# Add-residual RMSNorm on one core: three fixed 64 KiB slots per partition, 8 rows per tile, and every transfer in one queue in a fixed order

## The chip, the cores and the metric

The kernel runs on one core of one Trainium2 chip. The time is that of the device in microseconds (us). The profile shows one execution; its span is about 2 us shorter than the measured time (3762.5 against 3764.65 us before, 3732.7 against 3734.45 us after). Lower is better. A core has a VectorE (DVE in the profile), a ScalarE (ACT), a GpSimd (POOL), a SyncE (SP, which only issues transfers here) and 16 DMA engines by the profile's page, whose queue table has all 1612 MB that the kernel before moves.

## The reference

```python
x        : (32, 2048, 2048) float32        # 65536 rows of 2048
residual : (32, 2048, 2048) float32
gamma    : (2048,) float32, all ones;  eps = 1e-6

z   = x + residual
rms = sqrt(mean(z ** 2, axis=-1, keepdims=True) + eps)
out = z / rms * gamma
```

Each of the three large tensors has 536.87 MB. Each is moved once, so any kernel moves 1610.6 MB.

## The kernel before

A tile is 128 partitions of 2 consecutive rows: 16 KB per partition, 2 MB in all, 256 tiles. Loads are issued by SP, stores by ScalarE; pools of 6 and 4 buffers decide when a load may start.

```python
R = 2
x_t = x_f.rearrange("(n p r) m -> n p r m", p=P, r=R)        # r_t and o_t alike
...
nc.sync.dma_start(out=gamma_tile, in_=gamma.partition_broadcast(P))      # 1 MB
...
xio = ctx.enter_context(tc.tile_pool(name="xio", bufs=6))
rio = ctx.enter_context(tc.tile_pool(name="rio", bufs=4))
...
for i in range(n_tiles):
    x_tile = xio.tile([P, R, D], fp32)
    r_tile = rio.tile([P, R, D], fp32)
    nc.sync.dma_start(out=x_tile, in_=x_t[i])
    nc.sync.dma_start(out=r_tile, in_=r_t[i])
    nc.vector.tensor_add(out=x_tile, in0=x_tile, in1=r_tile)
    for g in range(R):
        nc.scalar.activation(out=sq_junk, in_=x_tile[:, g, :], func=Square,
                             accum_out=ssq[:, g : g + 1])
    ...  # rms = Sqrt(ssq / D + eps) on ScalarE, rstd = 1 / rms on VectorE
    for g in range(R):
        nc.vector.scalar_tensor_tensor(   # row * rstd * gamma, in place
            ...)
    nc.scalar.dma_start(out=o_t[i], in_=x_tile)
```

## Time and profile before

| | before |
|---|---|
| time, median of 4 runs | 3764.65 us (3764.07 to 3765.12) |
| bytes moved, by the queue table | 1611.96 MB |
| VectorE busy, ScalarE busy | 62%, 29% |
| DMA engines | at 9 tenths or more in 39 of 40 slices |

From the profile's page of the kernel before: the span, VectorE's and ScalarE's busy time, the DMA share and the rate in 40 equal slices, the DMA queues (packets, MB, share of the 16 engines), and the chain of waits by engine.

```profile
span 3762.5 us, 4011 instructions
DVE 2322.1 (62%) x1025; ACT 1103.6 (29%) x1282; POOL 0.2 (0%) x4
...
DMA  9999999999999999999999999999999999999998
GB/s 416 431 430 431 431 430 431 430 431 430 430 431 431 430 431 431 431 431 430 431 431 430 431 431 431 430 431 431 430 431 430 431 431 430 431 430 431 430 431 356
DMA packets 110767, 1611.96 MB, mean 428 GB/s; under 512 B 12304, under 2 KB 12304, under 8 KB 12304
...
q1 hardware_dynamic: 73872, 1074.82, 66.9%
q10 hardware_dynamic: 36864, 536.89, 33.3%
q14 instruction: 31, 0.25, 0.0%
...
DMA 91%; DVE 8%; issue 1%; SPq 0%; ACT 0%; DVEq 0%
```

The kernel is bound by its transfers from the second slice to the last but one, at a flat 430 to 431 GB/s. Only the first and the last slice are below that. q1 is the queue of the loads, q10 that of the stores, and q14 brings the engines' instructions, a quarter of a megabyte in 31 packets of 8 KB.

The end, in the table by stretches: from and to in us, length, busy us of each engine, clock, DMA share, GB/s.

```profile
60.00:200.00 140.00, 85.18 (x39) 38.79 (x46) 0.00 (x0) 1.00 1.01 431
...
3725.00:3730.00 5.00, 2.15 (x1) 0.00 (x0) 0.00 (x0) 1.00 0.96 413
3730.00:3735.00 5.00, 4.96 (x4) 2.66 (x3) 0.00 (x0) 1.00 0.19 82
3735.00:3740.00 5.00, 4.96 (x4) 1.64 (x3) 0.00 (x0) 1.00 0.59 249
3740.00:3745.00 5.00, 5.00 (x2) 0.00 (x0) 0.00 (x0) 1.00 1.01 429
3745.00:3750.00 5.00, 1.05 (x1) 3.88 (x4) 0.00 (x0) 1.00 0.55 236
3750.00:3755.00 5.00, 4.48 (x3) 0.42 (x3) 0.00 (x0) 1.00 0.00 0
3755.00:3762.50 7.50, 0.30 (x1) 0.00 (x0) 0.00 (x0) 1.00 0.66 280
```

The last 35 us hold about 16 us of missing transfer: 5 x (1 - 82/431) is 4 us in the stretch from 3730, and so on down the list. The timeline of the same end shows the adds of the last two tiles and the last store being issued (start, duration, what, and in brackets the idle time before it and what ended it):

```profile
3727.84 4.42 DVE L56 TENSOR_TENSOR x_tile<-x_tile,r_tile 128x4096 f32<-128x4096 f32 x1 [8.00 <-DMA r_tile<-in_residual_dram]
...
3741.64 4.42 DVE L56 TENSOR_TENSOR x_tile<-x_tile,r_tile 128x4096 f32<-128x4096 f32 x1
...
3755.33 0.34 ACTq L89 DMA_DIRECT2D out_dram<-x_tile  x1
```

From the last add to the last store there are 13.7 us of compute.

### The profile page before, as it was taken

What the parts mean: (1) busy time and instruction counts of PE and PEld (TensorE: products, weight loads), DVE (VectorE), ACT (ScalarE), POOL (GpSimd) and SP (SyncE); (2) the same over time, 40 slices, a digit from 0 to 9 for tenths busy, and PEclk for the clock granted to TensorE, in tenths of its full rate; (3) what the DMA queues carried; (4) which work ended last, traced back from release to release, by engine and by line L of the source; (5) the groups of instructions that cost most, each with busy time, mean ns of one, the idle gap of its engine ahead of it and who ended that gap; (6) DMA issues with size and microseconds to landing.
All of it is one profiled execution on the core that took longest, in us unless ns stands there. A gap on an engine that the chain in (4) does not pass through costs nothing.

```text
span 3762.5 us, 4011 instructions
## 1 busy us (share of the span) xinstructions
DVE 2322.1 (62%) x1025; ACT 1103.6 (29%) x1282; POOL 0.2 (0%) x4
## 2 busy tenths in 40 slices
DVE  5566656666566655666566655666556665566656
ACT  3232322323223232322323232232323222232322
POOL 0000000000000000000000000000000000000000
DMA  9999999999999999999999999999999999999998
GB/s 416 431 430 431 431 430 431 430 431 430 430 431 431 430 431 431 431 431 430 431 431 430 431 431 431 430 431 431 430 431 430 431 431 430 431 430 431 430 431 356
DMA packets 110767, 1611.96 MB, mean 428 GB/s; under 512 B 12304, under 2 KB 12304, under 8 KB 12304
## 3 DMA queue, kind: packets, MB, share of 16 engines
q1 hardware_dynamic: 73872, 1074.82, 66.9%
q10 hardware_dynamic: 36864, 536.89, 33.3%
q14 instruction: 31, 0.25, 0.0%
HBM read 1074.79 MB, written 536.87 MB: 428 GB/s over the span
## 4 chain that ended last, share of the span: by engine, by line
DMA 91%; DVE 8%; issue 1%; SPq 0%; ACT 0%; DVEq 0%
DMA r_tile<-in_residual_dram 53%; DMA x_tile<-in_x_dram 22%; DMA out_dram<-x_tile 15%; DVE x_tile L80 5%; DVE x_tile L56 3%; SPq L53 0%; ACT sq_junk L61 0%; DVE rstd L77 0%; DVEq L120 0%; SPq L54 0%; DVEq L56 0%; SPq L41 0%; ACT rms L69 0%
## 5 line engine op out<-in xcount | busy, mean ns | idle before, releaser
L56 DVE TENSOR_TENSOR x_tile<-x_tile,r_tile 128x4096 f32<-128x4096 f32 x256 | 1132.0, 4422 | 1413.1 <-DMA r_tile<-in_residual_dram 1413.0
L61 ACT ACTIVATE sq_junk<-x_tile 128x2048 f32<-128x2048 f32 x512 | 963.3, 1881 | 2637.9 <-DVE x_tile L56 2629.9
L80 DVE SCALAR_TENSOR_TENSOR x_tile<-x_tile,rstd,gamma_tile 128x2048 f32<-128x2048 f32 x512 | 1181.4, 2349 | 9.1
L61 ACT ACTIVATION_READ_ACCUMULATOR sq_junk<-x_tile 128x1 f32 x512 | 95.4, 186 | 0.0
L69 ACT ACTIVATE rms<-ssq,eps_tile 128x2 f32<-128x2 f32 x256 | 75.7, 296 | 8.2
L77 DVE RECIPROCAL rstd<-rms 128x2 f32<-128x2 f32 x256 | 40.3, 158 | 10.1 <-ACT rms L69 10.1
L61 ACT ACT_TABLE_LOAD x1 | 1.3, 1283 | 0.7 <-PEq L106 0.7
L69 ACT ACT_TABLE_LOAD x1 | 1.3, 1283 | 0.0
L43 DVE MEMSET eps_tile<- 128x1 f32 x1 | 0.1, 59 | 0.8 <-PEq L106 0.8
L106 POOL MEMSET const-uint8-127<- 128x1 uint8 x1 | 0.1, 102 | 0.0
L106 POOL MEMSET const-bfloat16-1.0<- 128x1 bf16 x1 | 0.1, 101 | 0.0
L106 POOL MEMSET const-float32-0.0<- 128x1 f32 x1 | 0.1, 98 | 0.2 <-issue 0.2
L106 POOL MEMSET const-float32-1.0<- 128x1 f32 x1 | 0.1, 98 | 0.0
## 6 DMA issues: line engine op xcount, KB each, us to landing
x_tile<-in_x_dram SPq DMA_DIRECT2D x256, 2048.0 KB, 34.3
r_tile<-in_residual_dram SPq DMA_DIRECT2D x256, 2048.0 KB, 37.3
out_dram<-x_tile ACTq DMA_DIRECT2D x256, 2048.0 KB, 14.4
gamma_tile<-in_gamma_dram SPq DMA_DIRECT2D x1, 1024.0 KB, 4.3
```

The source lines that it names most:

```text
L43: nc.vector.memset(eps_tile, float(eps))
L56: nc.vector.tensor_add(out=x_tile, in0=x_tile, in1=r_tile)
L61: nc.scalar.activation(out=sq_junk, in_=x_tile[:, g, :], func=mybir.ActivationFunctionType.Square, accum_out=ssq[:, g : g + 1],)
L69: nc.scalar.activation(out=rms, in_=ssq, func=mybir.ActivationFunctionType.Sqrt, bias=eps_tile, scale=inv_d,)
L77: nc.vector.reciprocal(out=rstd, in_=rms)
L80: nc.vector.scalar_tensor_tensor(out=x_tile[:, g, :], in0=x_tile[:, g, :], scalar=rstd[:, g : g + 1], in1=gamma_tile, op0=mybir.AluOpType. ...
L106: nc = _bacc.Bacc("TRN2", target_bir_lowering=False, num_devices=1)
```

## The change: its intent and the diff

The intent is to keep the 16 DMA engines busy with fewer and longer transfers, and to shorten the end. A tile becomes 8 rows, 64 KB per partition and 8 MB. There are two slots for z (x is loaded there, and the result is computed in place) and one for the residual. All large transfers go through SP's queue in the order store(i-1), residual(i+1), x(i+1): while one transfer runs, the wait that the next one needs has time to end. gamma is loaded into four partitions and spread over the others by VectorE.

```diff
-    R = 2
+    R = 8
+    H = R // 2
...
+    z_slots = [slots.tile([P, R, D], fp32, name=f"z{k}") for k in range(2)]
+    r_slot = slots.tile([P, R, D], fp32, name="r_slot")
...
-    xio = ctx.enter_context(tc.tile_pool(name="xio", bufs=6))
-    rio = ctx.enter_context(tc.tile_pool(name="rio", bufs=4))
+    def load_r(i):
+        nc.sync.dma_start(out=r_slot, in_=r_t[i])
+    def load_x(i):
+        z = z_slots[i % 2]
+        for h in range(2):
+            s = slice(h * H, (h + 1) * H)
+            nc.sync.dma_start(out=z[:, s, :], in_=x_t[i][:, s, :])
+    def store(i):               # whole tile; the last tile in two halves
+        ...
+    def compute(i):             # add, square, rms by halves; then scale by halves
+        ...
+    def load_gamma():
+        nc.vector.memset(gamma_tile, 0.0)
+        for q in range(4):
+            nc.scalar.dma_start(out=gamma_tile[32 * q : 32 * q + 1, :],
+                                in_=gamma.partition_broadcast(1))
+        nc.vector.stream_shuffle(gamma_tile, gamma_tile, [0] * 32)
...
+    load_r(0)
+    load_x(0)
+    load_gamma()
+    load_x(1)
+    compute(0)
+    load_r(1)
+    for i in range(1, n_tiles):
+        store(i - 1)
+        compute(i)
+        if i + 1 < n_tiles:
+            load_r(i + 1)
+            load_x(i + 1)
+    store(n_tiles - 1)
```

More of the change, by code (lines that the diff above doesn't have):

```diff
@@ L22 @@
     fp32 = mybir.dt.float32
+    Act = mybir.ActivationFunctionType
+    mult = mybir.AluOpType.mult
     x_f = x.flatten_outer_dims()
@@ L28 @@
     n_rows, D = x_f.shape
-    R = 2
+    R = 8
+    H = R // 2
     assert n_rows % (P * R) == 0
     n_tiles = n_rows // (P * R)
+    assert n_tiles >= 3
     x_t = x_f.rearrange("(n p r) m -> n p r m", p=P, r=R)
@@ L37 @@
     inv_d = 1.0 / float(D)
-    singles = ctx.enter_context(tc.tile_pool(name="singles", bufs=1))
-    gamma_tile = singles.tile([P, D], fp32)
-    nc.sync.dma_start(out=gamma_tile, in_=gamma.partition_broadcast(P))
-    eps_tile = singles.tile([P, 1], fp32)
-    nc.vector.memset(eps_tile, float(eps))
-    xio = ctx.enter_context(tc.tile_pool(name="xio", bufs=6))
-    rio = ctx.enter_context(tc.tile_pool(name="rio", bufs=4))
-    stats = ctx.enter_context(tc.tile_pool(name="stats", bufs=8))
-    psum = ctx.enter_context(tc.tile_pool(name="psum", bufs=1, space=bass.MemoryType.PSUM))
@@ L50 @@
-    for i in range(n_tiles):
-        x_tile = xio.tile([P, R, D], fp32)
-        r_tile = rio.tile([P, R, D], fp32)
-        nc.sync.dma_start(out=x_tile, in_=x_t[i])
-        nc.sync.dma_start(out=r_tile, in_=r_t[i])
-        nc.vector.tensor_add(out=x_tile, in0=x_tile, in1=r_tile)
-        sq_junk = psum.tile([P, D], fp32)
-        ssq = stats.tile([P, R], fp32)
-        for g in range(R):
-            nc.scalar.activation(
-                out=sq_junk,
-                in_=x_tile[:, g, :],
-                func=mybir.ActivationFunctionType.Square,
-                accum_out=ssq[:, g : g + 1],
-            )
-        rms = stats.tile([P, R], fp32)
-        nc.scalar.activation(
-            out=rms,
-            in_=ssq,
-            func=mybir.ActivationFunctionType.Sqrt,
-            bias=eps_tile,
-            scale=inv_d,
-        )
-        rstd = stats.tile([P, R], fp32)
-        nc.vector.reciprocal(out=rstd, in_=rms)
-        for g in range(R):
-            nc.vector.scalar_tensor_tensor(
-                out=x_tile[:, g, :],
-                in0=x_tile[:, g, :],
-                scalar=rstd[:, g : g + 1],
-                in1=gamma_tile,
-                op0=mybir.AluOpType.mult,
-                op1=mybir.AluOpType.mult,
-            )
-        nc.scalar.dma_start(out=o_t[i], in_=x_tile)
@@ new lines @@
+    slots = ctx.enter_context(tc.tile_pool(name="slots", bufs=1))
+    stats = ctx.enter_context(tc.tile_pool(name="stats", bufs=3))
+    psum = ctx.enter_context(tc.tile_pool(name="psum", bufs=1, space=bass.MemoryType.PSUM))
+    z_slots = [slots.tile([P, R, D], fp32, name=f"z{k}") for k in range(2)]
+    r_slot = slots.tile([P, R, D], fp32, name="r_slot")
+    gamma_tile = slots.tile([P, D], fp32, name="gamma_tile")
+    eps_tile = slots.tile([P, 1], fp32, name="eps_tile")
+    sq_junk = psum.tile([P, D], fp32, name="sq_junk")
@@ new lines @@
+    nc.vector.memset(eps_tile, float(eps))
+    def load_r(i):
[6 more added lines that the diff above has]
+    def store(i):
+        z = z_slots[i % 2]
+        if i < n_tiles - 1:
+            nc.sync.dma_start(out=o_t[i], in_=z)
+            return
+        for h in range(2):
+            s = slice(h * H, (h + 1) * H)
+            nc.sync.dma_start(out=o_t[i][:, s, :], in_=z[:, s, :])
@@ new lines, in compute @@
+    def compute(i):
+        z = z_slots[i % 2]
+        rstds = []
+        for h in range(2):
+            s = slice(h * H, (h + 1) * H)
+            nc.vector.tensor_add(out=z[:, s, :], in0=z[:, s, :], in1=r_slot[:, s, :])
+            ssq = stats.tile([P, H], fp32, name=f"ssq{h}")
+            for g in range(H):
+                nc.scalar.activation(
+                    out=sq_junk,
+                    in_=z[:, h * H + g, :],
+                    func=Act.Square,
+                    accum_out=ssq[:, g : g + 1],
+                )
+            rms = stats.tile([P, H], fp32, name=f"rms{h}")
+            nc.scalar.activation(out=rms, in_=ssq, func=Act.Sqrt, bias=eps_tile, scale=inv_d)
+            rstds.append((rms, stats.tile([P, H], fp32, name=f"rstd{h}")))
+        for h in range(2):
+            rms, rstd = rstds[h]
+            nc.vector.reciprocal(out=rstd, in_=rms)
+            for g in range(H):
+                row = z[:, h * H + g, :]
+                nc.vector.scalar_tensor_tensor(
+                    out=row,
+                    in0=row,
+                    scalar=rstd[:, g : g + 1],
+                    in1=gamma_tile,
+                    op0=mult,
+                    op1=mult,
+                )
@@ new lines, in load_gamma @@
+    def load_gamma():
+        nc.vector.memset(gamma_tile, 0.0)
+        for q in range(4):
+            nc.scalar.dma_start(
+                out=gamma_tile[32 * q : 32 * q + 1, :], in_=gamma.partition_broadcast(1)
+            )
+        nc.vector.stream_shuffle(gamma_tile, gamma_tile, [0] * 32)
[11 more added lines that the diff above has]
+            load_x(i + 1)
```

## The prediction

> **What bounds it now.** The transfers. The page's slices show the 16 DMA engines at 9 tenths or more in 39 of 40 slices, moving 430 to 431 GB/s from the second slice to the last but one; VectorE is busy 62%, ScalarE 29%. VectorE's idle time (1413 us) waits for the residual load. The chain of waits is 91% DMA. [...]
>
> **What isn't at full rate.** (a) Start: the stretches show the first bytes at about 1.8 us. (b) End: the last slice has 356 GB/s, a loss of about 16 us against 431. The timeline shows why: the last 2 MB tiles are added, squared and scaled after all loads are done, with gaps between stores (82 GB/s at 3730 to 3735 us, none at 3750 to 3755). (c) gamma costs 1 MB, 2.4 us. [...]
>
> **What the change does.**
> - gamma: four 8 KB loads instead of 1 MB: about -2.4 us. Memset and shuffle run while the first 16 MB load; free.
> - Transfers of 8 MB (residual, output) and 4 MB (x halves): 256 instead of 769. [...] steady rate 431 -> 433 to 434 GB/s; -20 to -25 us. My least certain gain.
> - End: the last loads are followed in the queue by the store of tile 62 (19.4 us), under which the last tile is added and half scaled. Estimate from durations: second add ends about 11 us after the last load ([...]add 2 x 4.42), four scalings (4 x 2.32) end at about 20 us, so the first half store starts 2 to 3 us late, the second nearly without gap[...]. Tail loss about 4 instead of 16 us.
> - Compute per tile: VectorE 17.7 + 18.8 = 36.5 us, ScalarE about 17 us, under 58.1 us of transfers.
> - Fixed order with three slots: the next residual needs both adds, ready about 11 us after x lands, while the store in front takes 19.4 us. x's slot needs the store landed, while the residual load takes 19.4 us. The queue should never run dry.
>
> Sum: transfers 3714 to 3721, start 2, end 4, and 2.2 us between span and time: about 3726 us (-1.0%).
>
> **Chances.** Range 3706 to 3765. Faster by over 2%: 0.01; within 2%: 0.93; slower: 0.06.
>
> **What would show it.** Last slice near 430 GB/s; steady slices 433 to 434; packets down to a third or fewer; ScalarE's queue nearly empty; VectorE still 62%, its idle time in few, long waits for x.
>
> **What would make it wrong.** [...] If the steady 431 GB/s doesn't depend on transfer size, the gain shrinks to 15 us. If pieces of 64 KB spaced over 8 MB suit the HBM worse, or the engines drift apart by over 8 us, the residual load comes late and the rate falls below 431.

## The result, and the profile after

| | before | after |
|---|---|---|
| time, median of 4 runs | 3764.65 us | 3734.47 us (3733.57 to 3734.64) |
| ratio to before, 95% interval | | 0.992 (0.9906 to 0.9934) |
| span of the profile | 3762.5 us | 3732.7 us |

The change saves 30 us, 0.8%: within 2%, as predicted; the predicted time was 3726 us, 8.5 us too low and inside its range. A ratio here is the mean time of one kernel's fast runs over that of the other's of the same rounds, so not quite the ratio of the medians that are quoted.

The same lines of the page after (page, kernel after):

```profile
span 3732.7 us, 2427 instructions
DVE 2298.0 (62%) x772; ACT 1066.4 (29%) x1154; POOL 0.2 (0%) x4
...
GB/s 425 414 437 430 435 433 431 435 435 432 433 431 435 436 430 437 429 436 433 431 436 430 437 432 431 437 430 439 430 432 434 432 437 431 430 435 436 431 435 389
DMA packets 37035, 1610.82 MB, mean 432 GB/s; under 512 B 4116, under 2 KB 4116, under 8 KB 4116
...
q1 hardware_dynamic: 37008, 1610.63, 99.9%
q14 instruction: 19, 0.16, 0.0%
```

The slices now move about 433 GB/s, with a third of the packets. Two slices stand out, the second (414) and the last (389). The table by stretches, kernel after:

```profile
60.00:200.00 140.00, 90.81 (x31) 33.53 (x37) 0.00 (x0) 1.00 1.00 423
...
150.00:3650.00 3500.00, 2159.32 (x726) 1004.82 (x1087) 0.00 (x0) 1.00 1.00 433
...
3700.00:3705.00 5.00, 4.96 (x4) 3.71 (x4) 0.00 (x0) 1.00 0.61 262
3705.00:3710.00 5.00, 5.00 (x3) 4.90 (x7) 0.00 (x0) 1.00 0.15 66
3710.00:3715.00 5.00, 4.96 (x4) 0.00 (x0) 0.00 (x0) 1.00 0.74 315
3715.00:3720.00 5.00, 5.00 (x3) 0.00 (x0) 0.00 (x0) 1.00 0.97 419
3720.00:3725.00 5.00, 0.04 (x1) 0.00 (x0) 0.00 (x0) 1.00 0.98 419
3725.00:3732.70 7.70, 0.00 (x0) 0.00 (x0) 0.00 (x0) 1.00 0.79 340
```

Between 60 and 200 us the rate is 423 and not 433, a loss of about 3 us that the kernel before does not have there. And the end has a hole of some 8 us from 3702 to 3712.

A sum for both kernels makes the shares visible. The steady rate is worked out from the trace's packets that end between 200 and 3600 us (their bytes over 3400 us); bytes over that rate is the time that the transfers need; the rest of the span is start and end. A packet of the kernel after carries up to 64 KB, so its rate is good to about 0.1 GB/s and its sums to about 1 us.

| | bytes | steady rate | transfers | rest of the span |
|---|---|---|---|---|
| before | 1611.96 MB | 430.6 GB/s | 3743.2 us | 19.3 us |
| after | 1610.82 MB | 433.1 GB/s | 3719.0 us | 13.7 us |
| difference | | | -24.2 us | -5.6 us |
| predicted for after | | 433 to 434 | 3714 to 3721 us | 6 us |

So the rate came as predicted, and nearly all that was missed is in start and end.

**What the landings say.** Each large transfer leaves 16 semaphore records in the trace, and the queue table has 16 packets under 512 B for each (12304 for 769 transfers before). They are read here as one record of each DMA engine, at the time when its share has landed. So read, they show something that no view of the page shows: how far the engines stand apart. These are the largest lags behind the median engine in a stretch of the trace (from and to in us, about), for the slowest four engines, in us (worked out from those records):

```
                   slowest   2nd   3rd   4th
before  1000-1500      8.0   7.4   7.2   0.9
before  3500-3720     19.7  19.6  18.5   1.8
after   1000-1500      4.5   2.7   2.3   1.7
after   3500-3720      7.7   6.7   5.3   1.4
```

Three of the 16 engines fall behind steadily, in both kernels. In the kernel before they are up to 19.7 us late in the last stretch, and 13.6 us for the very last load. That is the 82 GB/s: 13 engines had finished their loads by 3729 us, and three still loaded until 3740.5. In the kernel after, the three are 5 to 8 us late, and they are what fills the stretch at 66 GB/s.

From about 830 us on, the lag of the slowest engine of the kernel after doesn't grow evenly. It steps by nearly 1 us, each time within a few us of a packet of the instruction queue. The first four of six such steps:

```
instruction packet at   slowest engine's lag, transfer before -> after it
 837 us                 2.6 -> 3.5
1351 us                 3.6 -> 4.5
1932 us                 4.6 -> 5.5
2514 us                 5.5 -> 6.4
```

The last three are 581 us apart, ten tiles of 58.1 us, in which VectorE is given about 120 instructions. Before 837 us the lag had grown to 2.6 us without a step of that size, so these packets go with most of the 7.7 us, not with all of it. Another engine steps by about 0.6 us at ScalarE's rhythm; a third drifts by about 0.1 us per tile with no steps.

From here there were these theories:

- *Pieces*: the steady rate rose because an engine's share is cut into fewer contiguous pieces. Rivals: fewer transfers; or the single queue.
- *Slowest engine*: the end is set by the DMA engine that is furthest behind, and the lag comes from instruction fetches. Rivals: the end is set by the compute of the last tile (the reading of the prediction); or fetches cost nothing.
- *Start*: the missing 3 to 4 us near 100 us come from the order of the first loads. Rival: a gap at the start is hidden by the lag at the end.

### The profile page after: what moved, and what is told of

It reads as the page before. It is cut to its first block, busy times and chain, and to the rows that moved or that the text cites. A ratio compares the mean times of both kernels' runs of the same rounds, so it can differ in the third digit from the quotient of the medians.

```text
span 3732.7 us, 2427 instructions
## 1 busy us (share of the span) xinstructions
DVE 2298.0 (62%) x772; ACT 1066.4 (29%) x1154; POOL 0.2 (0%) x4
## 2 busy tenths in 40 slices
DMA packets 37035, 1610.82 MB, mean 432 GB/s; under 512 B 4116, under 2 KB 4116, under 8 KB 4116
## 4 chain that ended last, share of the span: by engine, by line
DMA 66%; another core or an unknown queue 16%; DVE 16%; SPq 1%; ACT 0%; issue 0%; DVEq 0%
DMA z<-in_x_dram 64%; DVE z L80 15%; DMA out_dram<-z 1%; DVE z L97 1%; DMA r_slot<-in_residual_dram 1%; SPq L64 1%; SPq L58 0%; ACT sq_junk L83 0%; DVE rstd L94 0%; DVEq L158 0%; ACT L90 0%; ACT rms L90 0%; DVEq L80 0%
## 5 line engine op out<-in xcount | busy, mean ns | idle before, releaser
L80 DVE TENSOR_TENSOR z<-z,r_slot 128x8192 f32<-128x8192 f32 x128 | 1112.5, 8692 | 1395.0 <-DMA z<-in_x_dram 1382.5
L83 ACT ACTIVATE sq_junk<-z 128x2048 f32<-128x2048 f32 x512 | 963.5, 1882 | 2635.0 <-DVE z L80 2622.9
L97 DVE SCALAR_TENSOR_TENSOR z<-z,rstd,gamma_tile 128x2048 f32<-128x2048 f32 x512 | 1169.9, 2348 | 4.5
L83 ACT ACTIVATION_READ_ACCUMULATOR sq_junk<-z 128x1 f32 x512 | 95.8, 187 | 0.0
L90 ACT ACTIVATE rms<-ssq,eps_tile 128x4 f32<-128x4 f32 x128 | 38.1, 298 | 4.1
L94 DVE RECIPROCAL rstd<-rms 128x4 f32<-128x4 f32 x128 | 21.9, 171 | 0.1
```

The costliest lines, as they stand in the source:

```text
L80: nc.vector.tensor_add(out=z[:, s, :], in0=z[:, s, :], in1=r_slot[:, s, :])
L83: nc.scalar.activation(out=sq_junk, in_=z[:, h * H + g, :], func=Act.Square, accum_out=ssq[:, g : g + 1],)
L90: nc.scalar.activation(out=rms, in_=ssq, func=Act.Sqrt, bias=eps_tile, scale=inv_d)
L94: nc.vector.reciprocal(out=rstd, in_=rms)
L97: nc.vector.scalar_tensor_tensor(out=row, in0=row, scalar=rstd[:, g : g + 1], in1=gamma_tile, op0=mult, op1=mult,)
```

## The experiments

All of them gave correct results.

### e1_gamma: the gamma part alone, on the kernel before

```diff
-    nc.sync.dma_start(out=gamma_tile, in_=gamma.partition_broadcast(P))
+    nc.vector.memset(gamma_tile, 0.0)
+    for q in range(4):
+        nc.scalar.dma_start(out=gamma_tile[32 * q : 32 * q + 1, :],
+                            in_=gamma.partition_broadcast(1))
+    nc.vector.stream_shuffle(gamma_tile, gamma_tile, [0] * 32)
```

> The kernel before with the stream shuffle for gamma alone. Theory: it saves the 1 MB broadcast, 2.4 us at 431 GB/s, and nothing else: about 3762.3 us. Rival: the shuffle part is worth more because the first tile starts late behind it: 5 us or more.

Measured: 3763.44 us against 3764.53 us before in the same rounds, 1.1 us less (ratio 0.9997, interval 0.9982 to 1.0012). The gamma part is worth about one microsecond of the thirty. Less than the 2.4 us came through, and 1.1 us is no more than the spread of e1's own runs (1.7 us).

### e2_pieces16 and e3_transfers2m: pieces or transfers

e2 keeps the changed kernel's transfers and their order, but gives a partition four pairs of rows that lie apart in memory, so that each 8 MB transfer has pieces of 16 KB. e3 keeps the layout, and cuts each transfer into ones of 2 MB, which have pieces of 16 KB too.

```diff
# e2_pieces16 (x_t, r_t and o_t; the SBUF side is viewed alike)
-    x_t = x_f.rearrange("(n p r) m -> n p r m", p=P, r=R)
+    x_t = x_f.rearrange("(n a p b) m -> n p a (b m)", a=R // 2, p=P, b=2)
# e3_transfers2m (load_r; load_x and store alike)
-        nc.sync.dma_start(out=r_slot, in_=r_t[i])
+        for j in range(0, R, 2):
+            nc.sync.dma_start(out=r_slot[:, j : j + 2, :], in_=r_t[i][:, j : j + 2, :])
```

> The changed kernel with the same transfers (8 and 4 MB, same order, same queue), but each cut into contiguous pieces of 16 KB in memory instead of 64 and 32 KB. Theory (cost per piece): the steady rate falls from 433 to about 431 GB/s, as before; time 3744 to 3751 us. Rival (cost per transfer, or the order of the queue): steady rate stays 433, time 3734 +- 2 us.

> The changed kernel with each transfer cut into 2 MB transfers of 16 KB pieces, same order in the same queue. If the cost is per piece: as the run with 16 KB pieces in large transfers, at most 5 us slower[...]. If the cost is per transfer: this one alone is slow (3745 us or more), the other not.

Measured: e2 3759.38 us (ratio 0.9987), e3 3764.91 us (ratio 1.0001). One stretch of each, in the table by stretches; first e2, then e3:

```profile
150.00:3650.00 3500.00, 2135.14 (x720) 988.77 (x1071) 0.00 (x0) 1.00 1.01 430
```

```profile
150.00:3650.00 3500.00, 2133.41 (x719) 988.76 (x1071) 0.00 (x0) 1.00 1.01 430
...
3725.00:3730.00 5.00, 5.00 (x1) 4.94 (x5) 0.00 (x0) 1.00 0.26 111
3730.00:3735.00 5.00, 4.96 (x4) 3.62 (x6) 0.00 (x0) 1.00 0.11 46
```

With 16 KB pieces the rate is 430 again, though the transfers are as long and as few as in the changed kernel. So the rate belongs to the pieces, not to the number of transfers or to the single queue. How the pieces lie in HBM seems to matter little: in e2 and in the kernel before, the pieces of neighbouring partitions follow one another, in e3 they lie 64 KB apart, and the rates are 430.2, 430.7 and 430.2 GB/s. What an engine does between two pieces, these runs don't show. The change itself couldn't tell pieces from transfers, as it makes both fewer by a factor of three.

The effect was larger than expected: 24.9 us instead of 10 to 17 (runs of different rounds; the kernel before took 3764.19 to 3764.65 us in all of them). An engine moves 32 pieces per tile in the changed kernel (8 of the residual, 16 of x, 8 of the result) and 96 in e2. Over 64 tiles that is 4096 more, so each costs 6.1 ns by this estimate. That is a hundredth of the 0.61 us that 16 KB take an engine at 1/16 of 430 GB/s.

e3 is 5.5 us slower still, a little over the author's estimate of 5 us at most, at the same steady rate. Its trace shows the slowest engine 16.6 us behind at the end, and e2's 7.3 us; e3 has 28 packets of instructions, e2 has 20. Its end has the long hole at 111 and 46 GB/s.

### e4_two_queues: the stores from ScalarE's queue

```diff
-            nc.sync.dma_start(out=o_t[i], in_=z)
+            nc.scalar.dma_start(out=o_t[i], in_=z)
```

> The changed kernel with the stores issued from ScalarE's queue instead of the one fixed queue. Theory (the store's place in the queue fills the time in which the next residual load waits for the adds): without it the DMA engines have nothing queued for about 12 us of each tile, the tile takes about 70 us instead of 58, time 4300 to 4600 us, with gaps in GB/s. Rival (which queue issues a transfer doesn't matter): 3734 +- 10 us.

Measured, one look: 4211.8 us, 477 us (13%) slower than the changed kernel, somewhat less than the 4300 to 4600 us expected. SP's own waits in e4 (who waited for whom, us in total, times, longest):

```profile
SPq L64 <- DMA out_dram<-z: 3469.2, 62, 57.8
SPq L58 <- DVE rstd L94: 546.6, 63, 27.8
```

My expectation named the wrong wait. The residual load's wait for the adds is short. The long one is that of the x load (L64) for the store out of its slot: 3469 us, where the kernel after has this:

```profile
SPq L58 <- DVE rstd L94: 1772.3, 63, 29.3
...
SPq L64 <- DMA out_dram<-z: 625.9, 62, 10.5
```

From its own queue, a store of e4 shares the engines with the loads. The one issued at 2035.4 us shared them with the end of a residual load (landed at 2043.6) and then with half of an x load; it landed at 2069.7 and that half at 2070.1. The next half of x was issued at 2069.7, with nothing left in front of it. The stretches of e4 show such a hole one tile earlier:

```profile
2005.00:2010.00 5.00, 1.81 (x1) 0.00 (x0) 0.00 (x0) 1.00 0.43 131
2010.00:2015.00 5.00, 5.00 (x1) 0.00 (x0) 0.00 (x0) 1.00 0.87 374
```

In the one queue the store comes first and lands while the residual load still runs (kernel after: the store by 2025.8 us on the last engine, the residual load by 2045.2). The edit did one thing more than its line says: the scheduler now puts half of the next x load before the residual load in SP's queue (the add at 2043.6 us follows a residual load issued at 2016.9, and the half of x that it adds to was issued before that, at 2008.4). So e4 shows that with three slots the order of service matters; it doesn't show what the store's queue alone is worth. The rate gained nothing from the second queue: e4 moved 383 GB/s from 100 to 3650 us. But the choice also changed the order of service, and here the two together cost 477 us.

### e5_tail_quarters: the last tile in quarters

```diff
+    def compute_last(i):        # add, square, rms, reciprocal, scale for rows 0-1, then 2-3, ...
+        ...
-        for h in range(2):
-            s = slice(h * H, (h + 1) * H)
+        for h in range(4):
+            s = slice(h * 2, (h + 1) * 2)
             nc.sync.dma_start(out=o_t[i][:, s, :], in_=z[:, s, :])
```

> The changed kernel, but the last tile is added, squared, scaled and stored in quarters, so that its first store can start about 8 us earlier. Theory (the run ends when the slowest DMA engine has done its share; that engine has no gap at the end, only the fast ones have): time falls by at most 2 us. Rival (the chain of the last tile's compute delays the end, as predicted): time falls by 5 to 8 us.

Measured: 3734.74 us (ratio 0.9921), the same as the changed kernel. The stretches at its end:

```profile
3700.00:3705.00 5.00, 5.00 (x3) 3.37 (x3) 0.00 (x0) 1.00 0.81 351
3705.00:3710.00 5.00, 5.00 (x3) 0.93 (x3) 0.00 (x0) 1.00 0.95 406
...
3725.00:3730.00 5.00, 0.00 (x0) 0.00 (x0) 0.00 (x0) 1.00 0.27 115
3730.00:3735.00 5.00, 0.00 (x0) 0.00 (x0) 0.00 (x0) 1.00 0.02 7
```

The hole at 66 GB/s is filled: 406. And not a microsecond is won. The missing rate turns up at the very end, 115 and then 7 GB/s, when most engines are done and the late ones still store: by the landings, 12 engines are done at 3726.2 us and the slowest at 3731.8, where the changed kernel ends as well (3731.7). So a shorter compute of the last tile wins nothing; the slowest DMA engine holds the end where it is.

In the changed kernel that engine works on both sides of the compute. The last add waits for its landing (timeline, kernel after):

```profile
3692.83 8.69 DVE L80 TENSOR_TENSOR z<-z,r_slot 128x8192 f32<-128x8192 f32 x1 [0.99 <-DMA z<-in_x_dram]
```

The median engine's share of that load had landed at 3685.0 us, the slowest's at 3692.8. From there the compute took 18.0 us to the first half store (issued at 3710.8), while the slowest engine was still at the store in front of it (landed at 3712.1). Its share of the half store landed 9.8 us later, hardly more than the 9.7 us that 4 MB take at 433 GB/s: it had no gap. The compute and the slowest engine were ready for the half store at nearly the same time, so shortening the compute alone can't help.

### e6_pool4096, e7_dve32 and e7b_dve16: more instructions that nothing waits for

```diff
# e6_pool4096
+    for _ in range(4096):
+        nc.gpsimd.memset(idle_tile, 0.0)
# e7_dve32, at the head of compute(i)
+        for _ in range(32):
+            nc.vector.memset(idle_tile, 0.0)
# e7b_dve16, behind each of a tile's two reciprocals
+            for _ in range(8):
+                nc.vector.tensor_copy(out=idle_tile, in_=rstd[:, 0:1])
```

> The changed kernel with 4096 one-element memsets on GpSimd, which does nothing else and which nothing waits for. Theory (instructions are fetched in pieces of 8 KB through the same DMA engines, and each fetch holds up one engine by 0.5 to 1 us): 32 more packets in the instruction queue, one DMA engine lags by 16 to 32 us, time +8 to +25 us. Rival (fetches cost nothing; the lag belongs to certain DMA engines): time within 2 us of 3734.5, spread of landings still about 8 us.

> The changed kernel with 32 one-element memsets per tile on VectorE, at a place where it is idle (2048 in all, about 2 us of VectorE per tile). Theory (fetches): 16 more packets in the instruction queue, the lag of VectorE's DMA engine grows from 8 to about 24 us, time +10 to +17 us. Rival: VectorE has 21 us of slack per tile, so time stays within 2 us of 3734.5.

> Mend of the run with 32 memsets, which the scheduler had moved in bunches ahead of the adds: here 16 one-element copies per tile stand behind the reciprocals by their data, 1024 in all, about 1.5 us of VectorE per tile, which has 21 us of slack. Theory (fetches): 8 more packets in the instruction queue, VectorE's DMA engine lags by about 8 us more (15 at the end instead of 7 to 8), time +6 to +9 us. Rival: time within 2 us of 3734.5 and the same lag.

Measured: e6 3753.12 us, e7b 3742.07 us; the changed kernel has 3734.47. The instruction queue of e6 and of e7b, against 19 packets in the changed kernel:

```profile
q14 instruction: 51, 0.42, 0.0%
```

```profile
q14 instruction: 27, 0.22, 0.0%
```

In e6, 32 more packets cost 18.6 us, 0.58 us each, though GpSimd does nothing for the result and VectorE's busy time stayed at 2298.0 us. The time came as expected, the lag didn't: instead of one engine 16 to 32 us late, the slowest was 11.5 us late at most, and 6.2 us at the end. The trace shows why. GpSimd ran all its memsets at once, from 0.7 to 642.5 us, with a packet about every 20 us. Between 144 and 318 us nine of them passed, and the slowest engine's lag rose from 3.0 to 8.1 us, 0.6 us for each, while all others stayed within 1.6 us. Then the lag rose more slowly, to 11.5 us near 610 us, and the rate fell. From the tenth slice on, when the memsets were done, the rate is back (page, e6; a slice is 94 us):

```profile
GB/s 424 410 435 426 420 424 405 424 424 437 431 435 433 432 435 434 431 435 432 437 432 431 437 431 436 434 431 435 434 432 434 431 436 434 430 435 431 438 431 397
```

In e7b, 8 more packets cost 7.6 us, 0.95 us each: the height of the steps in the lag of the changed kernel. That the time rises by as much as one engine's lag would, while VectorE and ScalarE have room, speaks for fetches that each hold up one DMA engine.

One part of the expectation failed: e7b's slowest engine was 7.7 us behind at the end, not 15. The lag stopped near 8 us (11.5 in e6), probably because the order allows little more: the next residual load was issued 8.7 us after x had landed on the last engine (kernel after, 2006.5 and 2015.2 us), at the start the first packet of data came 1.0 us after the first issue (0.7 and 1.7 us), and the store in front lasts 19.4 us. That leaves about 9.7 us, an estimate from these three; an engine that is later would make the other 15 wait, and the loss shows as steady rate: 432.2 GB/s in e7b (worked out as above) against 433.1, and the low slices of e6.

e7 was 3799.10 us, 64.6 us slower than the changed kernel where 10 to 17 were expected, and is not a measurement of fetches. The scheduler had moved the memsets, on which nothing depends, ahead of the adds in bunches of up to 225, and so delayed the adds of the early tiles (its slices 2 to 6 have 353 to 392 GB/s). e7b is its mend.

### e8_start and e9_start_tail: the first tiles

In the changed kernel the second residual load stands behind all of the second x tile, so both adds of tile 1 wait for it. The timeline of the kernel after:

```profile
70.59 0.35 SPq L69 DMA_DIRECT2D out_dram<-z  x1
83.10 17.29 DVE L80 TENSOR_TENSOR z<-z,r_slot 128x8192 f32<-128x8192 f32 x2 [12.54 <-DMA r_slot<-in_residual_dram]
...
100.42 0.33 SPq L58 DMA_DIRECT2D r_slot<-in_residual_dram  x1
```

The residual landed at 83.1 us. The store of tile 0 then had the engines for 19.4 us, until about 102 us; the third residual load was issued at 100.4 us, and its first packets came 1.0 us later, at 101.4. From 100.5 to 101.0 us about 2 of the 16 engines had a packet under way. e8 puts the last quarter of the second x tile behind the second residual load.

```diff
-    load_x(1)
+    for s in (slice(0, 4), slice(4, 6)):
+        nc.sync.dma_start(out=z_slots[1][:, s, :], in_=x_t[1][:, s, :])
     compute(0)
     load_r(1)
+    nc.sync.dma_start(out=z_slots[1][:, 6:8, :], in_=x_t[1][:, 6:8, :])
```

> The changed kernel, but the last quarter of the second x tile is queued behind the second residual load instead of before it. Theory (in the changed kernel the DMA engines run dry for 3.8 us between 75 and 150 us, because the third residual load waits for an add that waits for the second residual load): that loss goes, time 3730.5 +- 1 us, and the stretch from 60 to 150 us is at the steady 433 GB/s. Rival (a gap at the start is hidden, because the end is set by engines that lag anyway): within 1 us of the changed kernel.

> The same with the last tile in quarters as well. Theory (slowest DMA engine): no more than 1 us faster than the start order alone, about 3730 us. It should be the fastest of all, or equal to it.

Measured, with a 95% interval of the ratio to before: e8 3730.47 us, 0.991 (0.9895 to 0.9925); e9 3730.14 us, 0.991 (0.9895 to 0.9924). The stretch of e8 that had 423 GB/s in the kernel after:

```profile
60.00:200.00 140.00, 90.78 (x31) 34.25 (x38) 0.00 (x0) 1.00 1.01 433
```

The gap is gone, and the time fell by 4.0 us, as expected. In the kernel after, from the landing at 61.2 us to that at 142.4 (median of the 16 records), five transfers of 33.6 MB in all took 81.2 us, 3.7 us more than they need at 433.1 GB/s. So the loss at the start came through whole; the lag at the end didn't hide it. The order of three transfers at the start gave what the finer end could not. e8 and e9 are the fastest kernels, and the quarters of e9 add nothing that could be told from e8.

### e10_before_r4: longer pieces without the order

```diff
-    R = 2
+    R = 4
-    xio = ctx.enter_context(tc.tile_pool(name="xio", bufs=6))
-    rio = ctx.enter_context(tc.tile_pool(name="rio", bufs=4))
+    xio = ctx.enter_context(tc.tile_pool(name="xio", bufs=3))
+    rio = ctx.enter_context(tc.tile_pool(name="rio", bufs=2))
```

> The kernel before with 4 rows per tile and half as many buffers: 32 KB pieces, 4 MB transfers, still two queues, pools and no fixed order. Theory (cost per piece, 6 ns on each engine by the run with 16 KB pieces): steady rate about 432.5 GB/s, 19 us less of transfers; the end gets longer by about 8 us, as the last tile's chain doubles; time 3748 to 3760 us. Rival (the fixed order makes the rate): steady rate stays 430.6.

Measured: 3834.33 us (ratio 1.0185, interval 1.0168 to 1.0202), slower than before by about 1.9%; the expectation failed, and so did its rival. The stretch in the middle, and the longest of SP's own waits, of e10:

```profile
150.00:3650.00 3500.00, 2109.16 (x708) 973.79 (x1057) 0.00 (x0) 1.00 1.00 424
```

```profile
SPq L53 <- DMA out_dram<-x_tile: 2917.5, 125, 40.6
```

The rate fell to 424 GB/s. With half as many buffers of twice the size, x loads wait longer for stores that share the engines with other loads, as in e4: 2917.5 us in all, against 1601.8 in the kernel before. Longer pieces alone didn't pay here, where the buffers for them were taken from the depth of the queue; the changed kernel, with the fixed order, moved 433 GB/s.

## Why the prediction was right or wrong, point by point

- *Faster by over 2%: 0.01*: right, it was 0.8%. The chance was the author's estimate; the runs don't show a bound. The highest steady rate here, between 200 and 3600 us, was 433.3 GB/s (e9), at which 1610.6 MB take 3717 us.
- *Steady rate 433 to 434 GB/s, -20 to -25 us, "my least certain gain"*: right in size, -24.2 us together with gamma's megabyte. The rate was the author's estimate. The cost goes with the piece and not with the transfer: e2 gives all of the gain in rate back with unchanged transfers.
- *gamma -2.4 us*: about half came through, 1.1 us (e1).
- *Compute off the path, the queue never dry*: right in steady state (433 GB/s from 150 to 3650 us). The adds were done 8.7 us after x had landed on the last engine, where the author's estimate was 11. Wrong in the first tiles. There the second residual load lands late, and about 4 us are lost (e8). The "start 2" of the sum measured about 6: the 2 us that e8 still has in its first 200 us (429 GB/s there), and the 4 us that e8 wins.
- *Tail loss about 4 instead of 16 us*: the step that failed. The end lost about 8 us: 13.7 us of rest, less about 6 at the start. The prediction read the end of the kernel before as the compute of the last tiles. That fits about 10 of the 16 us, those after the last add began at 3741.6 us; the hole from 3730 to 3740, 6 us, is where three late DMA engines still loaded. For the kernel after, the chain of compute came as predicted: 18.0 us from the last landing to the first half store, against 2 x 4.42 + 4 x 2.32 = 18.1. What it had wrong is when that landing comes. It took one landing for all 16 engines; the adds wait for the slowest, 7.7 us behind the median, so the first half store started about 8 us late for most engines and not 2 to 3, and e5 shows that a shorter chain doesn't help.
- *What would show it*: packets down to a third (110767 to 37035), VectorE still at 62%, ScalarE's queue nearly empty (8 packets): right. VectorE's idle time is now put down to x, but not to few, long waits: 126, against 129 before. *Last slice near 430 GB/s*: wrong, 389, for the reason above.
- *What would make it wrong: a rate that falls below 431 GB/s*: didn't happen; the steady rate rose to 433.1. *Engines that drift apart by over 8 us*: they drifted by just that much (7.7 us), and e7b shows the rate beginning to fall there (432.2 GB/s).

The sum in short: the prediction had 3726 us, with 6 us for start and end; those took 13.7 us, and this is nearly all of the 8.5 us by which it was off.

## What to carry to other kernels

In this kernel, bound by its transfers, three places were left to look at: the length of the contiguous piece that each DMA engine moves (pieces of 16 KB instead of 64 and 32 KB cost 24.9 us, e2), stretches in which nothing is queued (4.0 us among the first tiles, e8, where the fixed order isn't yet in step), and the one engine that is last (7.7 us behind the median at the end). Compare the landings of the 16 engines before shortening the compute at the end: here one of them was late, the end belonged to it, and a shorter compute won nothing (e5). And with few, large slots, first work out for every transfer which wait it needs and which transfer runs meanwhile; a store in another queue changed that order here and cost 13%.

## What the runs show of fetches, pieces, late engines and queues

- The packets of the instruction queue are 8 KB (0.25 MB in 31; in e6, 32 more of them for 4096 more instructions), and in these kernels, bound by their transfers, each one cost 0.95 us for VectorE's (e7b) and 0.58 us for GpSimd's (e6), as if it held up one engine. Instructions that nothing waits for cost 18.6 us (e6).
- Piece length counts here: 16 KB pieces instead of 64 and 32 KB cost 24.9 us, an estimated 6.1 ns for each further piece on an engine (e2).
- SP and ScalarE issue every transfer of data, and still three of the 16 engines fall behind, up to 19.7 us before and 7.7 us after. In the kernel after, two of them step with the instruction packets. The third drifts by about 0.1 us per tile of 58 us; what slows it stays open, and so does which of the 16 it is, and whether the three of the kernel before, up to 19.7 us late, have the same causes.
- The spread of the transfers over two issuing engines didn't help the rate (383 GB/s in e4 against 433 in the kernel after), and with the order of service that it changed it cost 477 us.
